# A norm's inverse roots spread over the partitions through DRAM instead of by products on TensorE

## The chip, the core and the metric

The kernel runs on one core of a Trainium2 chip. The metric is the device time in microseconds of one execution; of several runs the median counts. The engines are named as the profile does: PE (TensorE, matmul) with PEld for its weight loads, DVE (VectorE), ACT (ScalarE), POOL (GpSimd), SP (SyncE, which here only issues DMAs).

## What is computed

Two blocks of a network on 512 tokens of 2048 channels, in float32. The first is a convolution branch and a differential attention of 8 heads; the second takes 256 tokens of context besides (ctx; the 512 are called lat, latent), and mixes them by a gated delta rule (GDN, 8 heads of 128 channels) and by RWKV-7 (16 heads of 64 channels). The change touches five norms over the channels of one head:

```python
def l2norm(t):                                   # GDN q and k; RWKV kk
    return t * lax.rsqrt(jnp.sum(t * t, axis=-1, keepdims=True) + EPS)
...
q = l2norm(qkv[:, :, 0]) * (GDN_HEAD ** -0.5)    # gn
k = l2norm(qkv[:, :, 1])                         # gn
...
kk = l2norm(rwkv_heads(k * k_k))                 # rn
...
o = rms_norm(o, subln_g) * (1.0 - lam_0)         # an, the attention's output
y = rmsnorm(o, norm_g).reshape(b, n, D_GDN) * jax.nn.silu(z.astype(jnp.float32))      # go
y = ((o - mu) * lax.rsqrt(var + GN_EPS)).reshape(b, n, D_RWKV) * gn_g + gn_b          # ro
```

## The kernel before

All activations lie with channels on the partitions and tokens along the row, a tile being 128 channels x 512 tokens (256 for ctx). A head of 128 channels is one tile (g = 1); two heads of 64 share one (g = 2). A sum over a head's channels is thus one across partitions, and so is the way back, when each token's inverse root has to reach all partitions of its head.

**Dense products.** Every projection is made in `products` (L120): a weight tile of 128 x 1024 (512 KB) is loaded to `wraw` (L127, three buffers), ACT rounds it to `whi` (L104), DVE takes the rest to `wlo` (L105, two buffers each), and PE makes 24 matmuls of 128 x 512 (L136). The dense matmuls have a priority in the framework's scheduler which lets them go ahead in bursts (12 at first, 6 in the second block), so that PE's order is dense work with the small matmuls of attention, GDN and RWKV set in between. Each engine takes its instructions in that order; one that waits holds up all behind it. All DMAs are issued by SP, in one order too: weight loads, spills to DRAM and their return.

**A norm** (`norm_bcast`, L803). The squares lie in a tile: `gc_th` in `gdn_prep` (the norms called gn, of GDN's q and k, 16 calls on lat), `go_t` in `gdn_out` (go, 8), `at_s` in the attention's heads (an, 8), `r_sq` in RWKV (rn, 8 on ctx and 8 on lat; ro, 8 on lat). One matmul per 128 tokens (L809) sums the squares: the result has tokens on the partitions, 128 x 4 or 128 x 8. DVE makes the inverse root there by eleven small instructions (`rsqrt`, L147 to L154; the last L154 writes the result, named gn_rs_y, go_rs_y and so on). Then, in `rsqrt_bcast` (L281), PE transposes it to a bank of PSUM (L288), ACT copies the 4 or 8 rows of 128 to SBUF, into the squares' own tile (L289), and PE spreads them over the partitions by one product for each row (L294; 4 or 8 of them, two passes each) into another bank. The consumer on DVE reads that bank: L559 for gn (gq, gk), L1105 for go (gz), L1220 for an (at_z), L848 for rn (rp_kk), L1071 for ro (rp_o). Two norms over all 2048 channels at the very end (`final`, wf) go the same way.

**Around it.** In GDN, while one head's chain of states runs (L722 to L745, PE and DVE in turn), the next head's q, k, v are made by dense products and prepared by `gdn_prep`; k is then transposed by L597, after L559. `gc_th` has one buffer, which also takes the tanh of the next silu (L185). In RWKV's latent part `r_sq` has one buffer, used by rn, by ro and for the load of z.

Of the kernel before, what the change touches and what calls it, by code (L numbers as in the profile page):

```python
# [9 lines left out]
F32 = mybir.dt.float32  # L10
# [8 lines left out]
EPS = 1e-6  # L19
# [45 lines left out]
def setup(ctx, tc, A):  # L65
    K = Ctx()
    nc = tc.nc
    K.nc, K.tc, K.A = nc, tc, A
    K.const = ctx.enter_context(tc.tile_pool(name="const", bufs=1))
    K.stp = ctx.enter_context(tc.tile_pool(name="stp", bufs=1))  # L70
    K.wp = ctx.enter_context(tc.tile_pool(name="wp", bufs=3))
    K.dram = ctx.enter_context(tc.tile_pool(name="dram", bufs=1, space=DRAM))
    K.pd = ctx.enter_context(tc.tile_pool(name="pd", bufs=2, space=PSUM))
    K.px = ctx.enter_context(tc.tile_pool(name="px", bufs=1, space=PSUM))
    K.pc = ctx.enter_context(tc.tile_pool(name="pc", bufs=2, space=PSUM))
    K.po = ctx.enter_context(tc.tile_pool(name="po", bufs=2, space=PSUM))
    K.dma = nc.sync
    K.fill = lambda: None
    K.burst = 12
    K.n_split = K.on_pool = 0  # L80
    K.cs, K.pre = {}, {}
    K.c, K.v = {}, {}
    load_consts(K, K.const, (("cst", CST, NCST, K.c), ("vec", VEC, NVEC, K.v)))
    K.cp = {}
    cpi = K.const.tile([128, 128], I32, name="cpi")
    nc.vector.tensor_copy(cpi, K.c["cpm"])
    for d in range(2):
        for l in range(2):
            K.cp[d, l] = cpi[:, 32 * (2 * d + l):32 * (2 * d + l) + 32]
    K.mod = {}  # L90
    for key, n in (("ada", 48), ("ada2", 48)):
        K.mod[key] = K.const.tile([128, n, 2], F32, name="mod_" + key)
    return K


def load_consts(K, pool, what):
    for name, lay, n, to in what:
        t = pool.tile([128, n], F32, name=name)
        K.nc.sync.dma_start(t, K.A[name])
        to.update({f: t[:, o:o + w] for f, (o, w) in lay.items()})  # L100


def split(K, hi, lo, src, eng=None):
    K.nc.scalar.copy(hi, src)  # L104
    (eng or K.nc.vector).tensor_tensor(lo, src, hi.bitcast(F32), op=ALU.subtract)  # L105
# [34 lines left out]
def rsqrt(K, pool, src, shape, a, eps, name, eng=None, exact=False):  # L140

    nc = K.nc
    eng = eng or nc.vector
    xh = pool.tile(shape, F32, name=name + "_xh")
    y = pool.tile(shape, F32, name=name + "_y")
    t = pool.tile(shape, F32, name=name + "_t")
    nc.vector.tensor_scalar(xh, src, 0.5 * a, 0.5 * eps, op0=ALU.mult, op1=ALU.add)  # L147
    eng.tensor_scalar(y.bitcast(I32), xh.bitcast(I32), -0.5, RSQ, op0=ALU.mult, op1=ALU.add)
    steps = [RSQ_STEP1, (1.0, 1.5), (1.0, 1.5)] if exact else [RSQ_STEP1, RSQ_STEP2]
    for m, b in steps:  # L150
        if eng is nc.vector:
            eng.scalar_tensor_tensor(t, y, -m, y, op0=ALU.mult, op1=ALU.mult)
            eng.tensor_tensor(t, t, xh, op=ALU.mult)
            eng.scalar_tensor_tensor(y, t, b, y, op0=ALU.add, op1=ALU.mult)  # L154
        else:
            eng.tensor_tensor(t, y, y, op=ALU.mult)
            eng.tensor_tensor(t, t, xh, op=ALU.mult)
            eng.tensor_scalar(t, t, -m, b, op0=ALU.mult, op1=ALU.add)
            eng.tensor_tensor(y, y, t, op=ALU.mult)
    return y  # L160
# [120 lines left out]
def rsqrt_bcast(K, pool, p, row, T, a, eps, name, px, g):  # L281


    nc = K.nc
    nt = T // 128
    y = rsqrt(K, pool, p[:, 0:g * nt], [128, g * nt], a, eps, name + "_rs", exact=True)
    p = px()
    nc.tensor.transpose(p[0:g * nt, 0:128], y, K.c["ident"])  # L288
    nc.scalar.copy(row[0:g * nt, 0:128], p[0:g * nt, 0:128])  # L289
    p = px()  # L290
    w = 128 // g
    for i in range(g * nt):
        u, t = i % g, i // g
        nc.tensor.matmul(p[w * u:w * u + w, 128 * t:128 * t + 128], start=True, stop=True, rhs=row[0:g * nt, 0:128],  # L294
                         lhsT=K.c["ident"][0:g * nt, i:i + 1].to_broadcast([g * nt, w]))
    return p[:, :T]
# [503 lines left out]
        yield  # L800


def norm_bcast(K, pool, sq, T, a, eps, name, px, g=2):  # L803


    p = px()
    w = K.c["bones"][:, 0:128:64] if g == 2 else K.c["ones"][:, 0:1]
    for t in range(T // 128):
        K.nc.tensor.matmul(p[:, g * t:g * t + g], lhsT=sq[:, 128 * t:128 * t + 128], rhs=w, start=True, stop=True)  # L809
    return rsqrt_bcast(K, pool, p, sq, T, a, eps, name, px, g)  # L810


def rwkv_pair(K, P, p, load, T, s, lora, R, finish=None):
# [32 lines left out]
    sq = norm.tile([128, T], F32, name="r_sq")  # L846
    nc.scalar.activation(sq, kk, AF.Square)
    nc.vector.tensor_tensor(kk, kk, norm_bcast(K, norm, sq, T, 1.0, EPS, "rn", pn), op=ALU.mult)  # L848
    cat = slice(128 * p, 128 * p + 128)
    up = pool.tile([96, 2, 2, 128], F32, name="rp_up")  # L850
# [740 lines left out]
def final(K, pool, act, xd, out, g2):  # L1591


    nc = K.nc
    n = len(act)
    k0 = 16 - n
    w = [pool.tile([128, 16, n, 128], F32R, name=f"fw{x}") for x in "hl"]
    x2 = pool.tile([128, 16, 512], F32, name="x2")
    per = 8 // n
    for i in range(0, 16, per):  # L1600
        raw = K.wp.tile([128, 8, 128], F32, name="wraw").rearrange("p (i k) c -> p i k c", k=n)
        nc.sync.dma_start(raw, K.A["wout"][i:i + per, :, k0:].rearrange("i p k c -> p i k c"))
        split(K, w[0][:, i:i + per], w[1][:, i:i + per], raw)
    for i in range(0, 16, 4):
        nc.sync.dma_start(x2[:, i:i + 4], xd[i:i + 4].rearrange("i p t -> p i t"))
    hs = [slice(0, 256), slice(256, 512)]

    def block(i, t, acc):
        ps = (K.pc.tile([128, 512], F32, name="pc") if i % 2 else K.pd.tile([128, 512], F32, name="pd"))[:, :256]
        for m in range(3 * n):  # L1610
            k, j = m // 3, m % 3
            nc.tensor.matmul(ps, lhsT=w[j // 2][:, i, k], rhs=act[k][j % 2][:, hs[t]], start=(m == 0),
                             stop=(m == 3 * n - 1))
        x = x2[:, i, hs[t]]
        nc.vector.scalar_tensor_tensor(x, ps, g2[:, 32 + i, 0:1], x, op0=ALU.mult, op1=ALU.add)
        eng = nc.vector if i in ((2, 5, 8, 11, 14, 15), (10, 13, 15))[t] else nc.gpsimd
        sq = pool.tile([128, 256], F32, name="f_sq", bufs=4)
        nc.scalar.activation(sq, x, AF.Square)
        if eng in acc:
            eng.tensor_tensor(acc[eng], acc[eng], sq, op=ALU.add)  # L1620
        else:
            acc[eng] = pool.tile([128, 256], F32, name="f_acc", bufs=4)
            eng.tensor_copy(acc[eng], sq)

    def rinv(t, acc):
        a, b = acc.values()
        nc.vector.tensor_tensor(a, a, b, op=ALU.add)
        po = lambda: K.po.tile([128, 512], F32, name="po")
        rf = norm_bcast(K, pool, a, 256, 1.0 / 2048, EPS, f"wf{t}", po, 1)
        rs = pool.tile([128, 256], F32, name="f_rs", bufs=2)  # L1630
        nc.scalar.copy(rs, rf)
        return rs

    def normed(i, t, rf):
        x = x2[:, i, hs[t]]
        if i % 3 == 2:
            nc.scalar.activation(x, x, AF.Copy, scale=K.v["fng"][:, i:i + 1])
            nc.gpsimd.tensor_tensor(x, x, rf, op=ALU.mult)
        else:
            nc.vector.scalar_tensor_tensor(x, x, K.v["fng"][:, i:i + 1], rf, op0=ALU.mult, op1=ALU.mult)  # L1640
        g = 4 - 2 * t
        if i % g == g - 1:
            nc.sync.dma_start(out[i - g + 1:i + 1, :, hs[t]].rearrange("i p t -> p i t"), x2[:, i - g + 1:i + 1, hs[t]])

    acc = {}
    for i in range(16):
        block(i, 0, acc)
    rf = rinv(0, acc)
    acc = {}
    for i in range(19):  # L1650
        if i < 16:
            block(i, 1, acc)
        if i > 2:
            normed(i - 3, 0, rf)
    rf = rinv(1, acc)
    for i in range(16):
        normed(i, 1, rf)


@with_exitstack  # L1660
def kernel(ctx, tc, A, out, parts="c12"):
    K = setup(ctx, tc, A)
    sb, se = ExitStack(), ExitStack()
    big = sb.enter_context(left(K, "big", 32))
# [151 lines left out]
```

## Time and profile before

| | us |
|---|---|
| median of 3 runs | 4013.55 (4008.08 to 4026.48) |
| the profiled run | 4016.7 |
| its span in the profile | 4014.9 |
| PE busy | 3771.6 (94%) |
| DVE busy | 2748.5 (68%) |
| ACT busy | 1362.0 (34%) |
| POOL busy | 478.7 (12%) |

The table's busy times come from the page's first part. PE's matmuls overlap each other and their ends are modelled, so PE's share is not that of its peak. The page then cuts the span in 40 slices, lists the DMA queues (495 MB in all, 123 GB/s on the mean), follows the chain of work that ended last, and gives the costliest groups of instructions and the DMAs with their times from issue to landing. The stages in order: the first block's modulation, its projections with the second block's ctx work, attention (up to about 1840 us), its output, GDN on lat (about 2300 to 3035), RWKV on lat (to about 3925), the last projection and the final norm.

### The profile page before, as it was taken

How to read it: one execution, taken by the hardware profiler on the slowest of the kernel's cores; microseconds unless marked ns; L12 is line 12 of the kernel's file. 1: busy time of each engine (PE TensorE's matmuls, PEld its weight loads, DVE VectorE, ACT ScalarE, POOL GpSimd, SP SyncE). 2: the span in 40 equal slices, each digit the busy share in tenths (PEclk: the TensorE clock that was granted, in tenths of full speed). 3: DMA queues.
4: the chain of work that ended last, by engine and by line, in shares of the span. 5: the costliest groups of instructions: out<-in, count | busy, mean ns of one | idle time of the engine just before them, and what ended most of it. 6: DMA issues, size and time to landing. Idle time of an engine off the chain costs nothing. (4 is left out here: it accounts for less than half of the span.)

```text
span 4014.9 us, 82142 instructions
## 1 busy us (share of the span) xinstructions
PE 3771.6 (94%) x33202; PEld 2894.3 (72%) x33202; DVE 2748.5 (68%) x7151; ACT 1362.0 (34%) x2707; POOL 478.7 (12%) x572
## 2 busy tenths in 40 slices
PE   8999879998999999999998799899999999999997
PEld 4676668886777776777886578777777777766776
DVE  3266797797777776644533976676667887877866
ACT  2311334322444343332322432232323444434433
POOL 0000221012100100000311200110001111110102
PEclk9999889999999999999999999998999999999998
DMA  8766435433324333524523232122223121222235
GB/s 318 264 216 202 159 128 169 150 110 103 120 95 129 115 115 106 168 88 158 205 104 119 103 97 77 65 72 67 85 80 103 64 73 56 73 67 88 97 123 203
DMA packets 211389, 495.08 MB, mean 123 GB/s; under 512 B 40640, under 2 KB 71872, under 8 KB 211008
## 3 DMA queue, kind: packets, MB, share of 16 engines
q1 hardware_dynamic: 211008, 489.82, 36.2%
q8 instruction: 261, 4.28, 0.4%
q14 instruction: 120, 0.98, 0.1%
HBM read 436.64 MB, written 53.09 MB: 122 GB/s over the span
## 5 line engine op out<-in xcount | busy, mean ns | idle before, releaser
L136 PE MATMUL pd<-big,whi 128*128 128x512 f32 x5344 | 1784.0, 411 | 10.6 <-ACT big L331 8.0
L136 PEld LDWEIGHTS pd<-big,whi 128*128 128x128 f32 x5344 | 978.2, 192 | 271.3 <-issue 30.9
L136 PE MATMUL pd<-big,wlo 128*128 128x512 f32 x2800 | 1118.2, 399 | 6.5 <-DVE wlo L105 6.2
L104 ACT CAST whi<-wraw 128x1024 fp32r<-128x1024 f32 (+2 forms) x500 | 506.8, 1014 | 1205.6 <-PE pd L136 1121.5
L105 DVE TENSOR_TENSOR wlo<-wraw,whi 128x1024 fp32r<-128x1024 f32 (+2 forms) x483 | 577.8, 1196 | 347.1 <-ACT whi L104 315.2
L136 PEld LDWEIGHTS pd<-big,wlo 128*128 128x128 f32 x2800 | 537.7, 192 | 130.4 <-DVE wlo L105 9.9
L136 PE MATMUL pd<-hc,whi 128*128 128x256 f32 x1184 | 233.7, 297 | 18.0 <-ACT gc_up L541 7.0
L136 PEld LDWEIGHTS pd<-hc,whi 128*128 128x128 f32 x1184 | 192.5, 199 | 22.8 <-ACT gc_up L541 7.4
L136 PE MATMUL pd<-hc,wlo 128*128 128x256 f32 x592 | 174.9, 296 | 23.3 <-DVE wlo L105 19.6
L136 PE MATMUL pd<-ext,whi 128*128 128x512 f32 x512 | 184.3, 400 | 3.7 <-DVE ext L105 3.7
L1133 DVE SCALAR_TENSOR_TENSOR cv_y<-cv_up,vec,cv_y 128x512 f32<-128x512 f32 x240 | 180.5, 752 | 4.4
L136 PE MATMUL pd<-fa,whi 128*128 128x512 f32 x448 | 149.3, 414 | 0.3 <-DVE wo L1520 0.2
L136 PEld LDWEIGHTS pd<-hc,wlo 128*128 128x128 f32 x592 | 117.4, 198 | 28.9 <-DVE wlo L105 23.3
L1029 ACT ACTIVATE rg_zw<-rg_H,rg_wc 64x64 f32<-64x64 f32 x320 | 104.7, 343 | 53.1 <-DVE rg_H L1047 46.5
L136 PEld LDWEIGHTS pd<-ext,whi 128*128 128x128 f32 x512 | 97.1, 190 | 28.0 <-DVE ext L105 5.0
L1047 DVE SCALAR_TENSOR_TENSOR rg_H<-pc,rg_wc,rg_zw 64x64 f32<-64x64 f32 x320 | 90.5, 283 | 34.4 <-PE pc L1039 25.3
L221 DVE SCALAR_TENSOR_TENSOR ada_ev<-wraw,cs_ada,ada_ev 128x512 f32<-128x512 f32 x120 | 92.5, 771 | 25.1 <-DMA wraw<-in_wada_dram 23.7
L546 DVE SCALAR_TENSOR_TENSOR gc_y<-gc_up,vec,gc_y 128x512 f32<-128x512 f32 (+1 forms) x160 | 106.3, 665 | 2.5
L916 POOL TENSOR_TENSOR rg_bk<-rg_th,rg_L 64x512 f32<-64x512 f32 x48 | 67.3, 1401 | 299.9 <-ACT rg_L L895 224.8
L136 PEld LDWEIGHTS pd<-fa,whi 128*128 128x128 f32 x448 | 80.2, 190 | 20.2 <-DVE fa L105 1.0
L1424 POOL TENSOR_TENSOR sgl<-sgl 128x512 f32<-128x512 f32 x16 | 34.9, 2182 | 470.7 <-ACT whi L104 463.6
L964 PE MATMUL px<-rg_C,rg_bk 64*128 64x128 f32 x512 | 89.5, 303 | 1.0 <-issue 0.7
(575 smaller groups left out, 5673.3 us busy)
## 6 DMA issues: line engine op xcount, KB each, us to landing
wraw<-in_w_dram SPq DMA_DIRECT2D x372, 512.0 KB, 3.6
wraw<-in_wada_dram SPq DMA_DIRECT2D x192, 512.0 KB, 4.4
wraw<-in_wo_dram SPq DMA_DIRECT2D x32, 512.0 KB, 3.4
sgl<-sgd SPq DMA_DIRECT2D x48, 256.0 KB, 3.4
wraw<-in_wout_dram SPq DMA_DIRECT2D x20, 512.0 KB, 4.1
wraw<-in_w_dram SPq DMA_DIRECT2D x32, 256.0 KB, 3.5
sgd<-msg SPq DMA_DIRECT2D x32, 256.0 KB, 3.5
wraw<-in_wco_dram SPq DMA_DIRECT2D x16, 512.0 KB, 3.5
```

Of the source, the lines that this page charges most:

```text
L104: K.nc.scalar.copy(hi, src)
L105: (eng or K.nc.vector).tensor_tensor(lo, src, hi.bitcast(F32), op=ALU.subtract)
L136: nc.tensor.matmul(ps[:, :T], lhsT=a[:, k], rhs=b, start=(n == 0), stop=(n == 3 * (k1 - k0) - 1))
L221: nc.vector.scalar_tensor_tensor(ev, raw[:, k], cs[:, kk, 0:1], ev, op0=ALU.mult, op1=ALU.add)
L546: nc.vector.scalar_tensor_tensor(y, up[:, t:t + T], w[:, t:t + 1], y, op0=ALU.mult, op1=ALU.add)
L916: nc.gpsimd.tensor_tensor(bk[uq, :, u], th[uq], F[uq], op=mul)
L964: nc.tensor.matmul(pg[:, m], lhsT=bk[q, 4 * r + m].rearrange("p x c -> p (x c)"), rhs=C[q, 4 * r + m, u], start=True, stop=True, tile_posi ...
L1029: nc.scalar.activation(zw[hv[u], d], H[hv[u], ms[d], u], AF.Copy, scale=wn[hv[u], 4 * d + mn])
L1047: nc.vector.scalar_tensor_tensor(Hn[hv[u], 4 * d + mn, u], pc3[hv[u], 2, d], wn[hv[u], 4 * d + mn], zw[hv[u], d], op0=mul, op1=ALU.add)
L1133: nc.vector.scalar_tensor_tensor(y, up[:, t:t + 512], w[:, t:t + 1], y, op0=ALU.mult, op1=ALU.add)
L1424: nc.gpsimd.tensor_tensor(g, g, q, op=ALU.add)
```

## The change

`norm_bcast` gets an argument `dma`, true for all calls but the two of the final norm. Sums and root stay. The root's tile (tokens on partitions) is then written to a tile in DRAM, one DMA per head in it, through a view that puts the token's index along the row: each element is a piece of 4 bytes, 512 a write (256 on ctx). One more DMA per head reads the row back, repeated over that head's partitions (128 of them, or 64), into the tile that held the squares. That tile is returned, and the consumer reads it from SBUF in place of a bank of PSUM. The read waits for the write. All are issued by SP.

```diff
-def norm_bcast(K, pool, sq, T, a, eps, name, px, g=2):
+def norm_bcast(K, pool, sq, T, a, eps, name, px, g=2, dma=True):
 
 
     p = px()
     w = K.c["bones"][:, 0:128:64] if g == 2 else K.c["ones"][:, 0:1]
-    for t in range(T // 128):
+    nt = T // 128
+    for t in range(nt):
         K.nc.tensor.matmul(p[:, g * t:g * t + g], lhsT=sq[:, 128 * t:128 * t + 128], rhs=w, start=True, stop=True)
+    if dma:
+        y = rsqrt(K, pool, p[:, 0:g * nt], [128, g * nt], a, eps, name + "_rs", exact=True)
+        K.n_norm += 1
+        d = K.dram.tile([g, T], F32, name=f"nb{K.n_norm}")
+        for u in range(g):
+            K.dma.dma_start(d[u].rearrange("(t c) -> c t", c=128), y[:, u:g * nt:g])
+        for u in range(g):
+            w = 128 // g
+            K.dma.dma_start(sq[w * u:w * u + w], d[u].partition_broadcast(w))
+        return sq
     return rsqrt_bcast(K, pool, p, sq, T, a, eps, name, px, g)
 
 
@@ -1626,7 +1637,7 @@
         a, b = acc.values()
         nc.vector.tensor_tensor(a, a, b, op=ALU.add)
         po = lambda: K.po.tile([128, 512], F32, name="po")
-        rf = norm_bcast(K, pool, a, 256, 1.0 / 2048, EPS, f"wf{t}", po, 1)
+        rf = norm_bcast(K, pool, a, 256, 1.0 / 2048, EPS, f"wf{t}", po, 1, False)
         rs = pool.tile([128, 256], F32, name="f_rs", bufs=2)
         nc.scalar.copy(rs, rf)
         return rs
```

That changes 56 calls: 32 with one head (gn 16, go 8, an 8) and 24 with two (rn 16, ro 8). Away go 56 transposes, 56 copies of ACT and the products behind them; SP gets 80 writes and 80 reads. Lines behind L810 move by 11: the consumers L848, L1071, L1105 and L1220 are L859, L1082, L1116 and L1231 in the changed kernel.

The scheduler sets a new order. Three engines at one place, the norm of k for the fourth head of GDN (gn) with the norm of the third head's output (go). PE first, before: from the go root's transpose to the transposing matmuls of gk, L597.

```order
L288 MATMUL po_23816<-cst_78,go_rs_y_23803 4x128
L294 MATMUL px1_24031<-gc_th_24007,cst_78 128x128 x2
L294 MATMUL po_23819<-go_t_23795,cst_78 128x128 x4
L294 MATMUL px1_24031<-gc_th_24007,cst_78 128x128 x2
L751 MATMUL po_24578<-gd_egt_24177,S_3_0_5864 128x128
L136 MATMUL pd_24799<-big_20615,whi_24801 128x512
L136 MATMUL pd_24799<-big_20616,whi_24801 128x512
L136 MATMUL pd_24799<-big_20615,wlo_24802 128x512
L136 MATMUL pd_24799<-big_20621,whi_24801 128x512
L136 MATMUL pd_24799<-big_20622,whi_24801 128x512
L136 MATMUL pd_24799<-big_20621,wlo_24802 128x512
L597 MATMUL px0_24190<-cst_78,gk_24003 128x128 x4
```

Ahead of these stand the go sum (L809), the gn root's transpose and six dense matmuls. After, the last rows before L597:

```order
L136 MATMUL pd_24670<-big_20664,whi_24702 128x512
L136 MATMUL pd_24670<-big_20665,whi_24702 128x512
L136 MATMUL pd_24670<-big_20664,wlo_24703 128x512
L136 MATMUL pd_24670<-big_20670,whi_24702 128x512
L136 MATMUL pd_24670<-big_20671,whi_24702 128x512
L136 MATMUL pd_24670<-big_20670,wlo_24703 128x512
L597 MATMUL px0_24071<-cst_78,gk_23889 128x128 x4
L722 MATMUL pc_24438<-S_3_0_5864,gk_23889 128x128
L722 MATMUL pc_24438<-S_3_1_5866,gk_23889 128x128
```

The transposes and products are gone; 30 dense matmuls in a row, of which the last six are shown, stand between the go sum (with one L751 behind it) and L597, where there were twelve.

DVE at the same place, before: the last steps of the two roots and the consumers.

```order
L154 SCALAR_TENSOR_TENSOR gn_rs_y_24015<-gn_rs_t_24016,gn_rs_y_24015 128x4
L152 SCALAR_TENSOR_TENSOR go_rs_t_23804<-go_rs_y_23803 128x4
L153 TENSOR_TENSOR go_rs_t_23804<-go_rs_t_23804,go_rs_xh_23802 128x4
L154 SCALAR_TENSOR_TENSOR go_rs_y_23803<-go_rs_t_23804,go_rs_y_23803 128x4
L1105 SCALAR_TENSOR_TENSOR gz_23245<-gz_23245,po_23819 128x512
L559 SCALAR_TENSOR_TENSOR gk_24003<-gk_24003,px1_24031 128x512
L1106 SCALAR_TENSOR_TENSOR gz_23245<-gd_o_23377,vec_80,gz_23245 128x512
L186 SCALAR_TENSOR_TENSOR gv_24108<-gc_th_24109,gc_y_24102 128x512
```

And after:

```order
L154 SCALAR_TENSOR_TENSOR gn_rs_y_23901<-gn_rs_t_23902,gn_rs_y_23901 128x4
L153 TENSOR_TENSOR go_rs_t_23700<-go_rs_t_23700,go_rs_xh_23698 128x4
L154 SCALAR_TENSOR_TENSOR go_rs_y_23699<-go_rs_t_23700,go_rs_y_23699 128x4
L559 SCALAR_TENSOR_TENSOR gk_23889<-gk_23889,gc_th_23893 128x512
L1116 SCALAR_TENSOR_TENSOR gz_23141<-gz_23141,go_t_23691 128x512
L105 TENSOR_TENSOR wlo_24773<-wraw_24771,whi_24772 128x1024
L1117 SCALAR_TENSOR_TENSOR gz_23141<-gd_o_23273,vec_80,gz_23141 128x512
L186 SCALAR_TENSOR_TENSOR gv_23989<-gc_th_23990,gc_y_23983 128x512
```

gk now comes ahead of gz, both read SBUF tiles that a DMA fills, and a weight's low half (L105) stands right behind them.

SP at the same place, before:

```order
L585 DMA gd_dd_24178<-gd_lat_20970 64x4x64 x4
L587 DMA gd_dx_24179<-gd_lat_20970 64x4x64 x2
L127 DMA wraw_24935<-in_w2_dram 128x1024
L127 DMA wraw_24981<-in_w2_dram 128x1024
L581 DMA gd_egt_25044<-gtd_lat_20971 128x2x512
L1503 DMA yd_20855<-gz_23245 128x512
L127 DMA wraw_25011<-in_w2_dram 128x1024
L127 DMA wraw_25562<-in_w2_dram 128x1024
```

And after, where nb26 is the root of the fourth head's q, nb27 that of its k and nb25 that of the third head's output (go):

```order
L127 DMA wraw_24801<-in_w2_dram 128x1024
L587 DMA gd_dx_24060<-gd_lat_20906 64x4x64 x2
L127 DMA wraw_24847<-in_w2_dram 128x1024
L816 DMA nb26_23814<-gn_rs_y_23801 128x4x1
L819 DMA gc_th_23793<-nb26_23814 128x512
L581 DMA gd_egt_24910<-gtd_lat_20907 128x2x512
L816 DMA nb27_23914<-gn_rs_y_23901 128x4x1
L816 DMA nb25_23712<-go_rs_y_23699 128x4x1
L819 DMA gc_th_23893<-nb27_23914 128x512
L819 DMA go_t_23691<-nb25_23712 128x512
L127 DMA wraw_24877<-in_w2_dram 128x1024
L1514 DMA yd_20791<-gz_23141 128x512
```

Each read stands behind its write; the two writes of the pair come first, then the two reads, and only then the next weight load.

## Rows read from the trace of the kernel before

**Rows 1.** The page's first part: busy us (share of span) and instructions of each engine.
```profile
PE 3771.6 (94%) x33202; PEld 2894.3 (72%) x33202; DVE 2748.5 (68%) x7151; ACT 1362.0 (34%) x2707; POOL 478.7 (12%) x572
```

**Rows 2.** Window table, GDN stage: us, busy by engine, PEclk, DMA share, GB/s.
```profile
core 0: us, PE busy (x) PEld busy (x) DVE busy (x) ACT busy (x) POOL busy (x), PEclk, DMA share, GB/s
...
2300.00:3035.00 735.00, 700.47 (x6556) 568.93 (x6555) 508.04 (x1569) 211.69 (x369) 64.92 (x150) 0.96 0.24 78
```

**Rows 3.** Waits: engine, line, waited for; us in total, times, longest us.
```profile
ACT whi L104 <- PE pd L136: 1121.5, 379, 13.7
...
PE pd L136 <- DVE wlo L105: 26.0, 22, 4.4
```

**Rows 4.** Window table of L294, then L288: whole span, and the final norm.
```profile
0.00:4014.00 4014.00, 67.61 (x584) 53.08 (x584) 0.96 0.37 123
3960.00:4014.00 54.00, 1.92 (x8) 1.44 (x8) 0.82 0.37 126
0.00:4014.00 4014.00, 16.54 (x58) 5.04 (x58) 0.96 0.37 123
3960.00:4014.00 54.00, 0.64 (x2) 0.16 (x2) 0.82 0.37 126
```

**Rows 5.** Idle of PE just before L288, then before L294: cause, us, times.
```profile
  issue: 11.8, 7
...
  DVE ro_rs_y L154: 2.3, 2
...
  issue: 6.8, 18
```

**Rows 6.** DMA issues: out<-in, KB each, median us from issue to landing.
```profile
gd_egt<-gtd_lat SPq DMA_DIRECT2D x8, 512.0 KB, 4.8
...
yd<-gz SPq DMA_DIRECT2D x8, 256.0 KB, 2.0
...
r_sq<-rl SPq DMA_DIRECT2D x8, 256.0 KB, 2.9
...
esl_lat<-gld_lat SPq DMA_DIRECT2D x1, 128.0 KB, 7.3
...
gld_ctx<-gg_gl SPq DMA_DIRECT2D x1, 0.5 KB, 3.6
gld_lat<-gg_gl SPq DMA_DIRECT2D x1, 1.0 KB, 1.6
```

**Rows 7.** SP's issues at L585, 256 pieces each: ns least/median/most, first and last start.
```profile
L585 SPq DMA_DIRECT2D gd_dd<-gd_lat x32: 585/616/1948, 2320.6 to 2892.5; - x32
```

**Rows 8.** Timeline, fourth head's q: start, us, engine, line; root's end and consumer.
```profile
2584.94 0.16 DVE L154 SCALAR_TENSOR_TENSOR gn_rs_y<-gn_rs_t,gn_rs_y 128x4 f32<-128x4 f32 x1
...
2590.24 0.68 DVE L559 SCALAR_TENSOR_TENSOR gq<-gq,px 128x512 f32<-128x512 f32 x1
```

**Rows 9.** Timeline, fourth head's k, third's go: root, consumers, L597; idle before in brackets.
```profile
2602.03 0.16 DVE L154 SCALAR_TENSOR_TENSOR go_rs_y<-go_rs_t,go_rs_y 128x4 f32<-128x4 f32 x1
...
2607.11 0.69 DVE L1105 SCALAR_TENSOR_TENSOR gz<-gz,po 128x512 f32<-128x512 f32 x1 [4.92 <-PE po L294]
...
2607.72 0.68 DVE L559 SCALAR_TENSOR_TENSOR gk<-gk,px 128x512 f32<-128x512 f32 x1
...
2609.16 0.60 PE L597 MATMUL px<-cst,gk 128*128 128x128 f32 x4
```

**Rows 10.** Timeline of PE: two neighbouring groups of dense matmuls, three apiece with wlo's.
```profile
2335.11 0.62 PE L136 MATMUL pd<-big,whi 128*128 128x512 f32 x2
...
2335.80 0.62 PE L136 MATMUL pd<-big,whi 128*128 128x512 f32 x2
```

**Rows 11.** Timeline of DVE, the last an: its root's end and its consumer.
```profile
1826.45 0.16 DVE L154 SCALAR_TENSOR_TENSOR an_rs_y<-an_rs_t,an_rs_y 128x4 f32<-128x4 f32 x1
1829.64 0.69 DVE L1220 SCALAR_TENSOR_TENSOR at_z<-po,at_z 128x512 f32<-128x512 f32 x1 [3.03 <-PE po L294]
```

**Rows 12.** Timeline of DVE, the first ro: its root's end and its consumer.
```profile
3182.45 0.15 DVE L154 SCALAR_TENSOR_TENSOR ro_rs_y<-ro_rs_t,ro_rs_y 128x8 f32<-128x8 f32 x1
...
3185.49 0.69 DVE L1071 TENSOR_TENSOR rp_o<-rp_o,po 128x512 f32<-128x512 f32 x1
```

More of the change, by code (lines that the diff above doesn't have):

```diff
@@ L79, in setup @@
     K.burst = 12
-    K.n_split = K.on_pool = 0
+    K.n_split = K.on_pool = K.n_norm = 0
     K.cs, K.pre = {}, {}
```

## The prediction

> **What bounds the kernel now.** I read the page's first part first: PE is busy 94% of the span [rows 1], and in the GDN stage of the latent tokens, where most of the changed norms lie, 700 of 735 us while DVE has 508 and DMA a quarter [rows 2]. So a microsecond of PE work that is removed is worth up to a microsecond of the end. Next the waits: PE hardly ever waits for a split weight (26 us in all for the low parts), whereas the cast of the next weight waits for PE 1121 us in 379 pieces [rows 3]. Weights are ahead of PE; what costs time is a matmul standing in PE's order whose input is late, since the dense matmuls behind it cannot pass. DVE, 69% busy in that stage, makes the low halves and all consumers of the norms, so it is the engine through which a late norm reaches PE.
>
> **What the change removes from PE.** The time table by line gives the products that spread the roots (L294) 67.6 us of busy PE and the transposes ahead of them (L288) 16.5 us; the two norms of the end, which keep the old way, have 1.9 and 0.6 of it [rows 4]. Removed: 67.6 - 1.9 + 16.5 - 0.6 = 81.6 us (term A). Almost all of it stands between dense matmuls with little idle time, so I count it whole.
>
> PE also sat idle just before these instructions. Before the transposes that was 29.6 us in six causes, from 11.8 (no visible wait) down to 2.3, the 3.7 of the end's norms and a rest of 0.6 left out; before the products 15.2 us in seven causes, 6.8 the largest, without the end's 1.0 [rows 5]. Together some 45 us. Such a wait goes only if what stands behind is ready, and behind many of these instructions stands the norm's own consumer. I take half: 22 us (term B); the bounds are 0 and 45.
>
> The 56 copies of a row by ACT go too: nothing, ACT is busy 34% [rows 1]. Two PSUM banks a norm come free earlier; I count nothing and leave it in the bounds of B. The sums over a head's channels and the small DVE steps stay.
>
> **What the change adds: a round trip.** After the root is ready on DVE, SP issues one write (two where a tile holds two heads) to DRAM, waits until it has landed, and issues a read that repeats a row over the partitions. No row of before shows such a write, whose pieces are 4 bytes, 512 of them (256 for the ctx tokens). Its bounds: plain writes to DRAM of 256 KB land 2.0 us after issue and the tiny write of the gates' last values 1.6 or 3.6; SP spends 0.62 us to issue a DMA of 256 pieces [rows 6, 7], so some 1.2 for 512, an estimate by proportion. I take 4.0 us: the 2.0 of a plain write, with 1.2 for the issue and 0.8 for the many pieces. For the read the bounds are 2.9 us (the same tile loaded with 256 KB) and 7.3 (the one load that repeats a 1 KB row over all partitions); the nearest is gd_egt, which repeats rows of 2 KB, two a partition, in 4.8 [rows 6]. With half its bytes I take 3.3. With 0.2 for the handover on SP a round trip is 7.5 us; about 8.5 where a second write stands behind the first, or where two norms come together. Bounds: 1.6 + 2.9 = 4.5 us, and 3.6 + 1.2 + 7.3 = 12.
>
> The Trainium skill ("DMA: Bandwidth & Descriptors", Rules for kernel authors) speaks against the write: a DMA whose last dimension is strided is lowered to one descriptor per element, and one should rearrange so that it is contiguous. No row of before shows what an element then costs. If it made the write land as late as the upper bound above, the sum would be that of the slower rival below.
>
> Now the same distance before, from root to consumer, and what is short:
> - gn of q, 8 calls. The fourth head's root ended at 2585.10 and its consumer began at 2590.24, 5.1 us later [rows 8]. Short: 7.5 - 5.1 = 2.4. DVE has steps of the state's chain to do in between (seven to nine rows in the order), so I charge 2.2 a call: 18 us.
> - gn of k and go, a pair in each head. At the fourth k the go root ended at 2602.19 and its consumer gz ran 4.9 us later, all of it a wait of DVE; gk followed at 2607.72 and the transposing matmuls of k (L597) at 2609.16 [rows 9]. In the new order the k read lands at about 2602 + 8.6 = 2610.6, gk takes 0.7, and L597 starts at about 2611.8, 2.6 us later than now: 8 x 2.6 = 21 us. PE's dense work ahead of L597 grows from 12 matmuls to 30, by 0.23 us each (two neighbouring groups of three start 0.69 apart) [rows 10] from 3 to 7 us; that is work pulled forward, no gain by itself, but it keeps PE from idling longer than before. DVE's next low half stands behind gz and is late too; PE has those 30 matmuls and most of a second weight split.
> - an, 8 calls. The last one waited 3.0 us from root to consumer [rows 11]: short by 4.5. The first half has other DVE rows in between, the second half next to nothing, and PE has dense blocks of the other branch; I let 0.3 of 8 x 4.5 through: 10 us.
> - ro, 8 calls with two heads: 2.9 us from root to consumer [rows 12], short by 8.5 - 2.9 = 5.6. The changed order has four to six large DVE rows in between; I let 0.35 of 45 through: 16 us.
> - rn: latent calls have three to seven large rows among 13 to 32 in between, near 8.5 us of DVE work; ctx calls less, with a shorter write. 2 us for all 16.
> Sum of term C: 18 + 21 + 10 + 16 + 2 = 67 us, an estimate, and the least certain.
>
> **The SP queue.** Each write stands in SP's queue ahead of weight loads, waits there for its root, and the read waits for the landing, some 5 us in which nothing is issued. At the fourth head's pair three whole weights that PE has not begun stand ahead of the load behind the reads, and PE takes 24 x 0.23 = 5.5 us for one; that load needs the 5 us and its own time to land. Covered; if SP came to the writes a whole weight too early, up to 5 us a head would show. The added bytes are 56 reads of 128 or 256 KB, 13.6 MB, at DMA a quarter busy [rows 2]: nothing. The tiles that receive the read are held until the consumer: gc_th also takes the tanh of the next block (before it was free at the products), r_sq the z load. ACT has the slack; counted with C.
>
> **The sum**, against the profiled run of 4016.7 us (span 4014.9; 3 us above the median 4013.55): -81.6 - 22 + 67 = -37, so 3980 for that run, and for a median 3977.
>
> **The rivals.**
> 1. *The forecast*: PE's work falls away, half of the gain is given back in later consumers. Terms A and C with their doubts put it between 3945 and 3995. Chance 0.42.
> 2. *The trip is short and hidden.* At 4.5 to 5 us gn and go lose nothing, ro and an keep some 8 us: 4013.55 - 82 - 22 + 8 = 3918; between 3910 and 3945. For it: writes to DRAM land in 2.0 [rows 6]; against it, the many pieces, and DVE's waits before gz. Chance 0.15. [...]
> 3. *The gain is eaten up.* One microsecond more of round trip costs, by the shares above, 8 x 0.5 (q) + 8 (k and go) + 8 x 0.4 (an) + 8 x 0.5 (ro), some 19 us. From 7.5 + 37/19 = 9.4 us nothing is left; 8.4 to 10.4 us gives 3994 to 4033, within 0.5%. Also here: PE's order holds it at the chain's end whatever it has less to do. Chance 0.23.
> 4. *Slower.* The small-piece write is the price: if it takes over 6 us, the trip reaches 11 to 12 us; DVE stands at gk and gz in every head with the next weight's low half queued behind, and PE, with 7 us of dense work ahead of it, waits for L597: 19 x (12 - 9.4) = +49, 4063; from 10.4 us on it is slower by over 0.5%. For it: DVE already waits 4.9 us at gz [rows 9]. Against it: no DMA of small pieces in the trace lands later than 3.6, the broadcast of 7.3 excepted [rows 6]. Chance 0.20.
> That the change doesn't do what it says has no place here: the transposes and products are gone from PE's order.
>
> **Chances and range.** A measurement of this kernel tells about 0.5%, 20 us, from no change: faster means below 3993. Rivals 1 and 2 lie there (0.57, less a tail of the forecast that ends just above 3993: 0.56), 3 is the same (0.23), 4 slower (0.21). The range leaves out the short end of rival 2 and the long end of 4: 3925 to 4045. The forecast's own range is 3945 to 3995.
>
> **What would show it.** Right: PE's busy time about 80 us lower; root to consumer of gn near 7.5 us; DVE's waits at L559, gz, at_z and rp_o on DMA, some tens of us in all. The write's landing time decides: below 2.5 us means rival 2, above 6 rival 4. PE's wait for wlo well above 26 us, or the casts waiting for weight loads, would show that SP or DVE passes the delay on to the dense products, which I counted at nothing; then the time lies above the range's middle even with a short trip.

## The result: slower by 8.2%

The changed kernel takes 4352.05 us (median of 6 runs, 4345.92 to 4359.7), the kernel before 4018.4 in the same rounds: ratio 1.082, 95% interval 1.080 to 1.084, 334 us more. The forecast was 3977, the range 3925 to 4045.

The page's first part of the changed kernel, as [rows 1]:

```profile
PE 3824.4 (88%) x32570; PEld 2932.3 (67%) x32570; DVE 2741.1 (63%) x7151; ACT 1352.5 (31%) x2651; POOL 481.1 (11%) x572
```

PE has 632 matmuls fewer and is 53 us longer busy: less work, done at a lower granted clock (0.917 on the mean, 0.961 before), with 526 us of idle time (4350.0 - 3824.4) where there were 243. To see where, here is a window table by stage of before (us, PE, PEld, DVE, ACT, POOL busy, granted clock, DMA share, GB/s). The bounds are the same events in both kernels; first the ctx and attention stage, then GDN, then RWKV on lat:

```profile
1023.00:1825.00 802.00, 785.59 (x7036) 578.89 (x7034) 562.67 (x1523) 307.64 (x713) 54.17 (x50) 0.98 0.35 116
...
2335.00:3023.00 688.00, 658.12 (x6374) 535.26 (x6373) 475.32 (x1468) 198.83 (x350) 64.38 (x146) 0.96 0.22 74
...
3042.00:3902.00 860.00, 820.35 (x10896) 609.45 (x10896) 670.16 (x1939) 360.03 (x877) 112.08 (x96) 0.95 0.24 78
```

and of the changed kernel:

```profile
1025.00:1906.00 881.00, 785.62 (x6897) 578.58 (x6895) 557.05 (x1519) 305.72 (x699) 52.33 (x50) 0.94 0.37 109
...
2426.00:3234.00 808.00, 666.86 (x6168) 540.57 (x6168) 480.48 (x1470) 194.81 (x327) 69.57 (x146) 0.89 0.25 71
...
3262.00:4224.00 962.00, 859.92 (x10635) 639.49 (x10636) 662.08 (x1938) 357.41 (x861) 111.26 (x96) 0.87 0.28 74
```

79, 120 and 102 us more: 301 of the 335 us by which the spans differ lie where the changed norms are, in all three stages. The granted clock falls with the idle time, from 0.95 to 0.87 in RWKV, so that 261 fewer matmuls there take 40 us more of busy time. The waits of DVE (engine and line, waited for; us, times, longest) name the place:

```profile
DVE gk L559 <- DMA gc_th<-nb: 77.5, 7, 13.5
DVE rp_kk L859 <- DMA r_sq<-nb: 73.5, 13, 8.2
...
DVE gq L559 <- DMA gc_th<-nb: 65.1, 8, 9.9
...
DVE at_z L1231 <- DMA at_s<-nb: 46.1, 6, 13.6
...
DVE rp_o L1082 <- DMA r_sq<-nb: 37.2, 7, 10.0
...
DVE gz L1116 <- DMA go_t<-nb: 24.0, 3, 13.5
```

That is 323 us in 44 waits; before, the same lines waited 44 us in all for their products on PE. One trip, the first q of GDN, in the timeline of the changed kernel, as [rows 8] (start, length, engine, line; in brackets the idle time before):

```profile
2427.45 0.16 DVE L154 SCALAR_TENSOR_TENSOR gn_rs_y<-gn_rs_t,gn_rs_y 128x4 f32<-128x4 f32 x1
...
2427.64 0.38 SPq L816 DMA_DIRECT2D nb<-gn_rs_y  x1
...
2437.32 0.33 SPq L819 DMA_DIRECT2D gc_th<-nb  x1
2442.60 0.69 DVE L559 SCALAR_TENSOR_TENSOR gq<-gq,gc_th 128x512 f32<-128x512 f32 x1 [9.59 <-DMA gc_th<-nb]
2443.33 0.63 ACT L185 ACTIVATE gc_th<-gc_y 128x512 f32<-128x512 f32 x1 [10.07 <-DVE gq L559]
...
2446.82 1.87 PE L810 MATMUL px<-cst,gc_th 128*128 128x1 f32 x8 [10.35 <-ACT gc_th L551]
```

The write goes out 0.03 us after the root, SP spends 0.38 us on it, and the read follows 9.7 us later, when the write has landed; 5.3 us more and the consumer runs: 15.0 us from root to consumer. Over all 56 norms the first read is issued 7.7 to 11.0 us after the first write, and from a root's end to its consumer it is 14.2 us on the mean, where it was 4.9. The delay goes on through `gc_th`, which has one buffer: ACT waits 10.07 us for gq until it can put the next tanh there, gk and its squares (L551) come after that, and PE, whose next matmul is their sum (L810), stands idle for 10.35 us. A window table of PE alone (us, PE busy, clock, DMA share, GB/s):

```profile
2426.00:2436.00 10.00, 10.00 (x45) 1.00 0.44 10
2436.00:2444.00 8.00, 0.47 (x3) 0.74 0.40 87
2444.00:2450.00 6.00, 3.19 (x12) 0.50 0.26 87
2450.00:2460.00 10.00, 10.00 (x38) 0.83 0.48 53
```

The granted clock was 1.00 ahead of the gap; in the 6 us in which PE starts again it is 0.50, 1.2 of 2.4 GHz. At the fourth head's k, as [rows 9], L597 waits for gk:

```profile
2649.34 0.16 DVE L154 SCALAR_TENSOR_TENSOR go_rs_y<-go_rs_t,go_rs_y 128x4 f32<-128x4 f32 x1
...
2661.95 0.69 DVE L559 SCALAR_TENSOR_TENSOR gk<-gk,gc_th 128x512 f32<-128x512 f32 x1 [12.46 <-DMA gc_th<-nb]
2662.56 0.68 DVE L1116 SCALAR_TENSOR_TENSOR gz<-gz,go_t 128x512 f32<-128x512 f32 x1
...
2662.79 1.09 PE L597 MATMUL px<-cst,gk 128*128 128x128 f32 x4 [6.32 <-DVE gk L559]
```

From the go root to L597 it was 7.0 us, it is 13.3.

### The profile page after: what moved, and what is told of

Its sections match the earlier page's. It is cut to its first block, busy times and chain, and to the rows that moved or that the text cites. A ratio compares the mean times of both kernels' runs of the same rounds, so it can differ in the third digit from the quotient of the medians.

```text
span 4350.0 us, 81052 instructions
## 1 busy us (share of the span) xinstructions
PE 3824.4 (88%) x32570; PEld 2932.3 (67%) x32570; DVE 2741.1 (63%) x7151; ACT 1352.5 (31%) x2651; POOL 481.1 (11%) x572
## 5 line engine op out<-in xcount | busy, mean ns | idle before, releaser
L136 PE MATMUL pd<-big,whi 128*128 128x512 f32 x5344 | 1823.2, 420 | 17.1 <-ACT big L331 8.0
L136 PEld LDWEIGHTS pd<-big,whi 128*128 128x128 f32 x5344 | 1007.9, 197 | 284.0 <-issue 30.2
L136 PE MATMUL pd<-big,wlo 128*128 128x512 f32 x2800 | 1137.7, 406 | 26.8 <-DVE wlo L105 26.0
L105 DVE TENSOR_TENSOR wlo<-wraw,whi 128x1024 fp32r<-128x1024 f32 (+2 forms) x483 | 576.4, 1194 | 307.0 <-ACT whi L104 277.4
L136 PEld LDWEIGHTS pd<-big,wlo 128*128 128x128 f32 x2800 | 549.7, 196 | 157.0 <-DVE wlo L105 31.9
L221 DVE SCALAR_TENSOR_TENSOR ada_ev<-wraw,cs_ada,ada_ev 128x512 f32<-128x512 f32 x120 | 91.6, 764 | 48.7 <-DMA wraw<-in_wada_dram 47.7
L975 PE MATMUL px<-rg_C,rg_bk 64*128 64x128 f32 x512 | 102.0, 331 | 9.7 <-DVE rg_C L978 7.7
L384 DVE COPY_PREDICATED iv_u<-cpi,px 128x256 f32<-128x256 int32 (+2 forms) x112 | 34.9, 339 | 113.7 <-PE px L381 87.6
```

The lines of the kernel that those rows point to most:

```text
L136: nc.tensor.matmul(ps[:, :T], lhsT=a[:, k], rhs=b, start=(n == 0), stop=(n == 3 * (k1 - k0) - 1))
L221: nc.vector.scalar_tensor_tensor(ev, raw[:, k], cs[:, kk, 0:1], ev, op0=ALU.mult, op1=ALU.add)
L975: nc.tensor.matmul(pg[:, m], lhsT=bk[q, 4 * r + m].rearrange("p x c -> p (x c)"), rhs=C[q, 4 * r + m, u], start=True, stop=True, tile_posi ...
```

## The experiments

**What makes the write long.** First the form of the write was changed, in two ways. In the first, PE's transpose and ACT's copy come back, and one write puts 4 or 8 rows of 128 into a tile of that shape:

```diff
-            K.dma.dma_start(d[u].rearrange("(t c) -> c t", c=128), y[:, u:g * nt:g])
...
+        K.nc.tensor.transpose(p[0:g * nt, 0:128], y, K.c["ident"])
+        K.nc.scalar.copy(sq[0:g * nt, 0:128], p[0:g * nt, 0:128])
...
+        K.dma.dma_start(d, sq[0:g * nt, 0:128])
```

> The changed kernel, but the root is transposed on PE and copied by ACT first, as before the change, so that the write to DRAM has 4 or 8 pieces of 512 bytes in place of 512 of 4 bytes; the read is that of the change. Theory A with the pieces as the cause of the long write: write to read issue falls from about 9.7 to 2 to 3 us, the round trip from 15 to 8 us, and the time from 4352 to between 4100 and 4200. Rival C (the write is long because it goes to DRAM and the read must wait for it, whatever its pieces): write to read issue stays above 7 us, and the time at 4330 or more.

Measured: 4031.37 us, ratio to before 1.001 (0.9988 to 1.0031). From write to read it takes 1.2 to 2.1 us in GDN, once 3.1. In the second, DVE transposes a tile of 128 x 32 in PE's place (m is the number of rows):

```diff
+        K.nc.vector.tensor_copy(yt[:, 0:m], y)
+        K.nc.vector.transpose(yo, yt)
...
+        for b in range(4):
+            K.dma.dma_start(d[:, 32 * b:32 * b + 32], yo[32 * b:32 * b + m])
```

> The changed kernel, but DVE transposes the root in blocks of 32 by 32 first (two more small DVE instructions a norm), so that four writes of 4 or 8 pieces of 128 bytes take the place of 512 pieces of 4 bytes; nothing goes back to PE. Theory A: write to read issue 3 to 4 us, round trip 8 to 9 us, 4100 to 4200 us. Rival C: 4330 or more. If the number of DMAs counts rather than their pieces, it is clearly slower than the run with one row write.

Measured: 4027.94 us, ratio 1.0012 (0.9993 to 1.0032). Both fall much further than expected: nearly the whole loss hangs on the form of the write, and rival C is out. That there are four DMAs in place of one does not show.

The same DMAs alone, behind the last store of before, where nothing else runs:

> The kernel before, with a chain of writes to DRAM and reads back appended behind its last store, each waiting for the one ahead, with nothing else under way: three each of 512, 256 and 128 pieces of 4 bytes, of one write of 4 pieces of 512 bytes, of four writes of 4 pieces of 128 bytes, and of 256 KB plain; the reads repeat a row over 128 partitions, the last three are plain. Pieces as the cause: about 9 us from write to read for 512, about 5 for 256, 3 for 128, 2 for the row. Rival D (contention with weight loads made the write long in the changed kernel): under 4 us for 512 here. For the read of a repeated 2 KB row: 5 us if the repetition is the cause, 3 us, as for the plain one, if it was contention.

SP's timeline, one write (to the DRAM tile mc) and one read behind it from each form, in the order 512, 256 and 128 pieces of 4 bytes, row, plain:

```profile
4014.01 0.36 SPq L1664 DMA_DIRECT2D mc<-wraw  x1
4023.49 0.33 SPq L1665 DMA_DIRECT2D wraw<-mc  x1
...
4053.16 0.36 SPq L1664 DMA_DIRECT2D mc<-wraw  x1
4062.12 0.33 SPq L1665 DMA_DIRECT2D wraw<-mc  x1
...
4090.52 0.32 SPq L1664 DMA_DIRECT2D mc<-wraw  x1
4097.51 0.32 SPq L1665 DMA_DIRECT2D wraw<-mc  x1
...
4118.24 0.26 SPq L1670 DMA_DIRECT2D mc<-wraw  x1
4119.41 0.33 SPq L1671 DMA_DIRECT2D wraw<-mc  x1
4122.39 0.26 SPq L1670 DMA_DIRECT2D mc<-wraw  x1
...
4147.45 0.32 SPq L1683 DMA_DIRECT2D mc<-wraw  x1
4149.46 0.32 SPq L1684 DMA_DIRECT2D wraw<-mc  x1
```

Contention (rival D) is out: the three writes of 512 pieces took 8.4 to 9.5 us with nothing else under way. But the length does not follow the count of pieces, as I had expected it to: it is 7.8 to 9.0 us for 256 and 7.0 to 7.5 for 128, against 1.2 for the row and 2.0 for 256 KB plain. A read of the repeated row takes 3.0 to 3.2 us behind the row write, 3.8 to 4.9 behind 512 small pieces. So the next chain varied the place and the size of 128 pieces:

> The kernel before, with a second chain behind its last store: writes from 128 partitions to DRAM, one piece of each, three times in each form, with a read behind each that waits: 4 bytes, neighbours 4, 64 and 512 bytes apart; 8, 16, 64 and 512 bytes side by side; and 4 bytes side by side from 32 partitions only. If small pieces in one line of DRAM get in each other's way: about 7 us for the first, 2 us when they lie 512 bytes apart, and shorter with the size of a piece. If a piece of 4 bytes as such is slow: 7 us at each distance. If the number of partitions counts: 7 us for pieces of 512 bytes too.

SP's timeline, pairs with 4 bytes and neighbours 4, 64 and 512 bytes apart, then with 8 and 16 bytes side by side:

```profile
4034.46 0.32 SPq L1665 DMA_DIRECT2D mc<-wraw  x1
4041.50 0.32 SPq L1666 DMA_DIRECT2D wraw<-mc  x1
...
4049.68 0.32 SPq L1665 DMA_DIRECT2D mc<-wraw  x1
4051.09 0.32 SPq L1666 DMA_DIRECT2D wraw<-mc  x1
...
4061.33 0.32 SPq L1665 DMA_DIRECT2D mc<-wraw  x1
4062.73 0.32 SPq L1666 DMA_DIRECT2D wraw<-mc  x1
...
4069.10 0.32 SPq L1665 DMA_DIRECT2D mc<-wraw  x1
4071.96 0.32 SPq L1666 DMA_DIRECT2D wraw<-mc  x1
...
4086.99 0.32 SPq L1665 DMA_DIRECT2D mc<-wraw  x1
4088.50 0.32 SPq L1666 DMA_DIRECT2D wraw<-mc  x1
```

4 bytes take 7.0 us side by side, and 1.4 at 64 bytes' distance as at 512; 8 bytes side by side take 2.6 to 3.2, and 16, 64 and 512 bytes 1.4 to 1.5. So neither the smallness of a piece nor the 128 partitions make a write slow by themselves: small pieces that lie close together in DRAM do, and then their number counts too (32 of them take 3.0). Why they do, no run shows. The changed kernel's view makes every one of its writes of that kind.

**What the long write costs.** Here the norms go the old way, with the change's writes and reads beside them, and nothing uses what is read. The reads bring only a part of the row, since with whole ones the tile finds no room in SBUF:

> The kernel before, norms the old way, and beside it every write of the change, with its 4-byte pieces, and a read behind each that waits for it, into a tile that nothing reads (for space the read takes only the first 128 tokens of each row, a quarter of the bytes or half for ctx). Theory A (the time is lost by consumers that wait for the round trip): within 20 us of before, 4000 to 4040 us. Rival B (SP's queue is held and 37000 small pieces load the DMA queues, so that weights come late): 4150 us or more.

Measured: 4164.89 us, ratio 1.0364 (1.0345 to 1.0382): 145 us with nobody waiting for the data. Theory A, that only waiting consumers cost time, failed; rival B's 4150 or more came true. The writes alone, with no reads:

> The kernel before, norms the old way, with the 80 writes of 4-byte pieces alone and no reads: SP waits for the root but for no landing. If the 145 us of writes and reads together came from the wait of a read for its write on SP: 4015 to 4045 us. If the pieces themselves slow other transfers: 4100 us or more.

Measured: 4133.52 us, ratio 1.0285 (1.0246 to 1.0324), 112 us: SP waits for no landing here, so most of it is not SP held by reads. The first ro in this run, from its timeline (DVE's and SP's rows for r_sq and rp_o): the z load is issued behind the two writes.

```profile
3230.44 0.92 SPq L817 DMA_DIRECT2D nb<-ro_rs_y  x2
...
3232.84 0.33 SPq L1265 DMA_DIRECT2D r_sq<-rl  x1
...
3244.76 0.69 DVE L1560 SCALAR_TENSOR_TENSOR rp_o<-rp_o,r_sq 128x512 f32<-128x512 f32 x1 [2.33 <-DMA r_sq<-rl]
```

DVE waits for that load until 3244.76, 11.9 us after its issue; in before these loads landed after 2.9 [rows 6]. Over the eight z loads DVE waits 28.2 us here, and 0.3 before. What is behind the small pieces in the queue comes late, read or not. To part this from SP's waits for the roots, the last variant changes addresses alone:

```diff
-        d = K.dram.tile([g, T], F32, name=f"nb{K.n_norm}")
+        d = K.dram.tile([g, T, 16], F32, name=f"nb{K.n_norm}")
...
-            K.dma.dma_start(d[u].rearrange("(t c) -> c t", c=128), y[:, u:g * nt:g])
+            K.dma.dma_start(d[u].rearrange("(t c) s -> c t s", c=128)[:, :, 0], y[:, u:g * nt:g])
```

> The kernel with the unread writes alone, but each 4-byte element goes to DRAM 64 bytes behind the one ahead in place of 4; the same number of DMAs and of pieces, and the same order on every engine, SP included. Measured alone such a write of 128 pieces took 1.4 us against 7.0. If the 112 us came from the time for which the writes occupy the DMA queues, with other loads behind them: 4020 to 4045 us. If they came from SP's waits for the roots, or from the number of pieces: 4100 us or more.

Measured: 4018.29 us, ratio 1.0006 (0.9986 to 1.0026). SP, DVE, ACT and POOL have the same instructions in the same order, and the 112 us are gone; a write now lands 1.7 to 2.6 us after its issue (medians by norm), and the z loads in 2.8. So the 112 us came from the writes' long landing, with other transfers behind them, and neither from SP's waits for the roots nor from the number of pieces.

Then SP itself: the change's DMAs on POOL's queue, by `K.nc.gpsimd.dma_start`.

> The changed kernel, its writes and reads issued by POOL in place of SP, everything else as it is: SP's order of weight loads is free of the waits for a root and for a landing. If the 145 us that the unread writes and reads cost came from SP being held: 4180 to 4260 us, the consumers' waits staying. If they came from the 4-byte pieces in the DMA queues: 4320 us or more. If POOL's issue is itself slower than SP's, the trip grows and the time can exceed 4352; the trace then shows the longer write.

Measured: 4415.35 us, ratio 1.0985 (1.0948 to 1.1022). Freeing SP brings nothing here: at the first three norms of GDN POOL's read follows its write after 8.5 to 11.1 us, and DVE's waits for the round trips grow to 406 us in six rows like those above. But POOL has work of its own behind these waits, so the run doesn't price SP's waits cleanly.

**What a long trip costs without small pieces.** This is the run with DVE's transposing, with copies from DRAM to DRAM ahead of the read, one and then four (shown):

```diff
+        for i in range(4):
+            e = K.dram.tile([m, 128], F32, name=f"nc{K.n_norm}_{i}")
+            K.dma.dma_start(e, d)
+            d = e
```

> The run with DVE's transposing, and one more step in the round trip: the row is copied once from DRAM to DRAM before it is read, some 2 us more. If the price is linear, 321 us for the 7.5 us that the changed kernel's trip is longer than that run's, 43 us for one: 4028 + 85, 4090 to 4130 us. If half of the norms still have cover at that length: 4040 to 4075 us.

> The run with DVE's transposing, its contiguous writes and no 4-byte piece, with four copies of the row from DRAM to DRAM in a chain ahead of the read, some 2 us each: the round trip is as long as the changed kernel's, 14 to 16 us, and SP is held as long, but no small piece is in the queues. If the changed kernel's 324 us above that run are 112 to 145 for the queues and the rest for waiting consumers: 4028 + 180 to 212, between 4190 and 4260 us. If the wait explains all and the queue's part is hidden behind it: 4330 or more. If the wait is cheap even at that length, as one copy's 26 us suggest (12 us for one): 4120 to 4150.

Measured: 4054.41 us (ratio 1.009, 1.0075 to 1.0105) and 4211.99 us (1.0496, 1.0462 to 1.053). The first lies in the band for norms of which half still have cover, the second in the band in which queues and waits both cost. From a root's end to its consumer it is 10.0 us on the mean without copies, 12.6 with one and 21.4 with four. So 2.6 us more cost 26 us, some 10 us for one, and 11.4 us more cost 184, 16 us for one (from write to consumer the first k takes 18.0 us instead of 6.7). With four copies the trips are longer than the changed kernel's, 14.2 on the mean, and yet the kernel is 140 us faster: the length of the trip alone does not make the loss. The scheduler knows of the copies and sets more work of DVE ahead of the consumers: they wait 137 us for the trips, against 323 in the changed kernel.

**What the work taken from PE is worth.** This variant leaves out the spreading: the tile is filled with one root of each partition.

```diff
...
+        K.nc.scalar.activation(sq, sq, AF.Identity, scale=0.0, bias=y[:, 0:1])
         return sq
```

> The changed kernel without any spreading: after the root, ACT writes the root of one token of each partition over the whole tile (one instruction) and the consumer goes on; the result is therefore another. No transposes, no products, no round trip: what the removal of the work on PE is worth at most. By terms A and B of the prediction: 4018 - 82 - 22, between 3890 and 3940 us. Rival E (PE is held by chains of PE and DVE in a fixed order, so that its work that goes away turns into idle time and a lower clock): 3970 us or more.

Measured: 3997.99 us against 4020.08, ratio 0.994 (0.9921 to 0.996): 22 us, not 104. Rival E holds. Its page's first part:

```profile
PE 3721.3 (93%) x32570; PEld 2857.8 (72%) x32570; DVE 2759.0 (69%) x7151; ACT 1382.0 (35%) x2707; POOL 486.5 (12%) x572
```

PE's busy time falls by 50 us, not by the 81.6 of the removed instructions, and its idle time, span less busy, rises from 243 to 276. Two things explain most of it. Neighbouring matmuls overlap the removed ones: without their rows PE's busy time in the trace of before would be 3710.2 us, only 61 less. And PE now waits for others, for low halves 19 us more than before (26.0 [rows 3]) and for POOL's rg_bk 12 us more; a row of before, then the two of this run:

```profile
PE px L942 <- POOL rg_bk L917: 9.7, 9, 2.1
...
PE pd L136 <- DVE wlo L105: 44.8, 28, 4.4
...
PE px L947 <- POOL rg_bk L922: 22.1, 17, 2.8
```

**Repairs.** These are two tries at a version that beats both. In the first each partition writes its tokens side by side, and the consumers read with a step:

```diff
-            K.dma.dma_start(d[u].rearrange("(t c) -> c t", c=128), y[:, u:g * nt:g])
+            K.dma.dma_start(d[u].rearrange("(c t) -> c t", t=nt), y[:, nt * u:nt * u + nt])
...
-        return sq
+        return sq.rearrange("p (c t) -> p t c", t=nt)
```

> The changed kernel with another order of the row in DRAM: each partition writes its 4 tokens side by side (128 pieces of 16 bytes; 8 bytes on ctx) and the consumers read the row with a step. No instruction more than in the changed kernel. The write measured alone took 1.4 us in this form against 7.8 to 9.5. If that is the whole cause: the level of the two runs with contiguous writes, 4010 to 4035 us, at best the 3998 of no spreading at all. If the consumers' stepped reading is slower on DVE, each by some tenths of a microsecond, still under 4060.

Measured: 4058.6 us, ratio 1.0083 (1.0058 to 1.0107): the loss shrinks from 334 to some 35 us, but doesn't end. The groups of DVE instructions (busy us, mean ns, idle before) show the step's price:

```profile
L559 DVE SCALAR_TENSOR_TENSOR gq<-gq,gc_th 128x512 f32<-128x512 f32 x8 | 8.6, 1069 | 3.9 <-DMA gc_th<-nb 3.9
...
L866 DVE TENSOR_TENSOR rp_kk<-rp_kk,r_sq 128x512 f32<-128x512 f32 x8 | 9.8, 1220 | 0.1
```

1.07 us (one of 2.03 lifts the second mean) for 0.68 to 0.69 before [rows 8, 9], about 0.4 x 48 = 19 us of DVE. Whether the rest of the 35 us has the same cause, no run shows. The second uses this form for attention and ctx alone:

> The 16-byte form for the attention's and the ctx norms only (16 calls), products on PE for all of GDN's and RWKV's on the latent tokens. In the run with DVE's transposing this stretch was 9 us shorter than before and the GDN stretch 12 us longer: 4005 to 4015 us, 5 to 15 below before. If the gain there was order and not work: 4020, no difference.

Measured: 4019.04 us, ratio 1.0002 (0.9984 to 1.002): no difference. With no spreading at all worth 22 us in the scheduler's order, little is left for any way of spreading, and no version here beats the kernel before.

## Why the prediction was wrong

**The write's landing, 4.0 us: the step that failed.** It was 7.7 to 11.0 us. Its upper bound, 3.6 + 1.2, came from rows of before in which pieces are few (the 64 pieces of 16 bytes, or 8, of the gates' last values) or lie as whole rows, and it weighed how many pieces there are, not how close they lie. The 3.6 us of the 8-byte pieces beside the 1.6 of the 16-byte ones in [rows 6], one DMA each, fit the same effect, 2.6 to 3.2 and 1.4 to 1.5 us in the chain: the row was there, and I took it for a spread. The rule of the Trainium skill that I weighed ("DMA: Bandwidth & Descriptors", Rules for kernel authors: a strided last dimension makes one descriptor per element; make it contiguous) gave the right advice; by these runs its reason is only half of it, since the same number of 4-byte elements 64 bytes apart cost nothing that shows (1.0006 of before). SP's issue stayed at 0.38 to 0.50 us (medians by norm), so the 1.2 us by proportion was wrong too.

**The read, 3.3 us.** It took 3.0 alone behind a row write and about 5 in GDN of the changed kernel. The round trip was 15 us at the first q, not 7.5, and beyond the upper bound of 12. Rival 4 had the mechanism, the places and its point ("if it takes over 6 us"), but a chance of 0.20 and too small a price: 4063.

**"ACT has the slack".** ACT had, but what waits behind `gc_th` on ACT is in PE's order: at the first q the held tile passed 10 us on to PE (L185, then L810).

**"Covered" for the queue.** I weighed only SP's waits and the added bytes. That each write takes 8 to 11 us to land and delays transfers behind it was no term; unread, the writes cost 112 us, and 145 with reads. The dense weights were covered nearly as said: the casts' waits for weight loads rose from 15.0 to 23.8 us. PE's for low halves rose from 26.0 to 47.2, the sign that I had named for a delay passed on; but it tells nothing, for with no spreading and no DMA it is 44.8. The loads that come late in the changed kernel are others: DVE waits 47.7 us for the modulation's weights, 23.7 before, and ACT 24.5 for one of RWKV's loads (lk), 10.9 before. The z load, late in the run with unread writes, costs 3.8 us here, where it is issued behind the reads; so what the writes cost unread need not be what they cost in the changed kernel.

**Terms A and B, -104 us.** They were 22 with no spreading at all. "A microsecond of PE work that is removed is worth up to a microsecond" held only as a bound. Counting the 81.6 us whole was wrong by the 20 in which neighbouring matmuls overlap them, and of what was left some 30 came back as waits for DVE's low halves and for POOL: "weights are ahead of PE" was true of the kernel before, but not once PE had less to do. (GDN has 24 of the 56 changed norms, the most of any stage, but not most of them.)

**Term C, 67 us at a trip of 7.5,** was too large as well: from no spreading to a sound write, with a first k of 6.7 us, it is 30 us (3998 to 4028). With a sound write the change is 1.001 of before: rival 3, "the gain is eaten up", would have been right at the trip that I forecast.

**The price per microsecond, 19 us,** was near: 10 to 16 in the runs with copies. On the changed kernel: 4028 with a sound write, then 8 us more of trip at 16 us, 130, and the queues, 112 to 145, make 4270 to 4303 of 4352. That these parts add up is assumed, and the last 50 to 80 us are not parted by a run. That its order sets consumers nearer behind the root (323 us of DVE's waits against 137) is the likeliest reason, argued and not shown.

**The clock** had no term. The changed kernel and the one with no spreading have the same 32570 matmuls; PE was busy with them for 3824.4 us at a granted clock of 0.917 in the one and 3721.3 at 0.957 in the other. These 103 us are part of the loss by every cause above, not one more.

## What to carry to other kernels

Before a transfer through DRAM is put in a path, look at how its pieces lie at the far end: the same 2 KB landed after 1.2 us as four rows and after 8.4 to 9.5 us as 512 neighbouring elements, and loads queued behind it came late. The cheap test is the DMA without a reader: whatever that costs is lost with nobody waiting for the data, and a kernel that skips the step altogether shows, ahead of all work on it, what there is to win (22 us here, of 82 us of instructions). A busy share of 94% is no proof that removed work shortens the span.

## What was not expected of the hardware

- 128 pieces of 4 bytes took 7.0 us to land side by side and 1.4 us at a distance of 64 bytes; 128 pieces of 8 bytes side by side took 2.6 to 3.2, of 16 bytes 1.4 to 1.5; 32 pieces of 4 bytes took 3.0.
- A read right behind such a write is slower too: 3.8 to 4.9 us against 3.0 to 3.2 for the same repeated 2 KB row.
- A DVE instruction on 512 columns with one operand read from SBUF with a step of four elements took 1.07 us in the median, against 0.69.
